# Attention scores of one head pair: 64-row matmuls in three products, or 128-row matmuls on stacked halves

## The chip, the core and the metric

The kernel runs on one core of one Trainium2 chip. TensorE multiplies matrices (a matmul needs a weight load, shown as PEld, and a moving operand), VectorE (DVE) and ScalarE (ACT) do elementwise work and read the results from PSUM, GpSimd (POOL) does a little elementwise work, and SyncE (SP) issues transfers, which 16 DMA engines carry out. Each engine works through its own list of instructions in a fixed order; semaphores make one wait for another. SyncE's list is a queue too: an issue that waits holds up the issues behind it.

The metric is the device time of one execution in microseconds. Executions differ a little: three runs of this kernel gave 2321.94, 2323.30 and 2325.07 us.

## What is computed

The reference is a trunk of two layers over 512 tokens of width 1024. Each layer has a gated feed-forward half step, a mixer, a second feed-forward half step and a gated embedding. The mixer of the first layer is a state-space scan, that of the second is neighbourhood attention on a grid of 8 rows by 64 columns. The change is inside that attention alone:

```
qkv = (h @ w_qkv).reshape(bsz, rows, GRID_W, 3, NA_HEADS, NA_HEAD_DIM)   # 16 heads of 64
q = rmsnorm(qkv[:, :, :, 0], q_norm) * (NA_HEAD_DIM ** -0.5)
k = rmsnorm(qkv[:, :, :, 1], k_norm)
s = q . k  over a window of 8 rows x 32 columns = 256 keys per block of 16 query columns
s = s + bias;  pr = softmax(s);  o = pr . v
```

There are 4 blocks of 16 columns by 8 rows, so 128 queries by 256 keys per block and head. A score is a sum over the 64 elements of a head.

Everything is in 32-bit floats. TensorE is used in a rounded form of them (fp32r), so the kernel splits each operand into a high part (rounded) and a low part (the rest), and adds three products: high with high, high with low, low with high.

## The kernel before

Activations lie with features on the 128 partitions and tokens on the free axis, as 8 tiles of 128 by 512. Weights come in units of 128 by 1024 (512 KB), loaded by SyncE (`load_unit`, L204), split into high and low by ScalarE (L221) and VectorE (L223), and used by `gemm`: 24 matmuls of 128 rows by 512 columns (L278, L281, L282), three products for each of 8 tiles. Up to three units wait as raw loads and up to three are split ahead.

In `attention` two heads share a tile of 128 partitions: head 0 of a pair on partitions 0 to 63, head 1 on 64 to 127. There are eight pairs, numbered j.

`keys` projects the key tiles (four early, four beside the loop), sums their squares (L1135), takes the reciprocal root on VectorE (L1139, on 8 partitions), writes it to DRAM (L1141), brings it back spread over the partitions (L1147), scales the keys (L1148) and splits them into a tile `kn` with a high and a low half (L1150, shown as L303 and L304). `kn` stays in SBUF, in the list `kz`, until its pair is done.

`project(j)` is a generator with four steps. It asks for the bias tables (L1166, two transfers of 384 KB, one for each head), runs the query projection in two halves, scales it (L1173), splits it into `qs[0]` (ScalarE, L1177) and `qs[1]` (VectorE, L1178), and then runs the value projection; beside it stands the reciprocal root of the query's norm (L1184 to L1188).

`attend(j)` runs one pair behind, beside `project(j + 1)`. `scores` takes two blocks of queries at a time and fills two PSUM banks, one for each head (L1209): for each block three products, each for both heads, so 12 matmuls with 64 rows, 128 query columns and 256 keys. The two heads' matmuls alternate in the program and use different rows of the array. `soften` adds the bias (L1219) and does the softmax (L1222 to L1234), `values` turns the values (L1243), `turn` the probabilities (L1252, L1254), and `weigh` multiplies both, with 64 output columns per matmul (L1263).

The order of each engine's list is not the program's. The framework that compiles the kernel places instructions on each engine by a planner: it goes by program order as a priority, by modelled durations and by which operands and tile slots are ready at the modelled time. So SyncE issues the bias of pair 1 in the same breath as that of pair 0, and a score block can be split by work that became ready in the planner's view. Tiles come from pools with a fixed number of slots: `hs` (8, for h, and in this stage for `qs`), `md` (24, of two halves each), `sq` (4), and five plus three PSUM banks.

At the start of the stage the eight tiles of h are parked in DRAM (L133), and fetched again at its end (L139) into the slots that `qs` used.

Of the kernel before, what the change touches and what calls it, by code (L numbers as in the profile page):

```python
# [14 lines left out]
P = 128  # L15
# [55 lines left out]
def trunk(ctx, tc, A, out):  # L71
# [1010 lines left out]
    def attention(norm, nxt):  # L1082
# [9 lines left out]
        def keys(js):  # L1092
# [50 lines left out]
            for i in range(4):  # L1143
                rb = sc()
                for a in range(2):
                    r_ = slice(a * 64, (a + 1) * 64)
                    sy.dma_start(out=rb[r_], in_=rkd[2 * i + a:2 * i + a + 1, :].to_broadcast([64, T]))  # L1147
                v.scalar_tensor_tensor(out=rb, in0=raw[i], scalar=gqk, in1=rb, op0=ALU.mult, op1=ALU.mult)  # L1148
                kn = md(F32R)
                split(kn, rb, None)  # L1150
                kz.append(kn)
                if js[0]:
                    yield
            yield
# [5 lines left out]

        def project(j):

            bias = []
            for a in range(2):
                bt = md().rearrange("p x k -> p (x k)")[:, :768].rearrange("p (x k) -> p x k", x=3)
                sy.dma_start(out=bt, in_=A["bias"][j, :, 3 * a:3 * a + 3, :])  # L1166
                bias.append(bt)
            pt, w = mm_bank(), unit()
            half_gemm(pt, w, 0)
            yield  # L1170
            half_gemm(pt, w, 1)
            qb = t2()
            v.tensor_mul(out=qb, in0=pt, in1=R)  # L1173
            qq = sc()
            s.activation(out=qq, in_=qb, func=AF.Square)
            qs = [bp.tile([P, T], F32R, name=nm("hs"), tag="hs", bufs=8) for _ in range(2)]
            s.copy(out=qs[0], in_=qb)  # L1177
            v.tensor_sub(out=qs[1], in0=qb, in1=qs[0])  # L1178
            yield
            pt, w = mm_bank(), unit()  # L1180
            half_gemm(pt, w, 0)
            pq = px_bank()
            for b in range(4):
                te.matmul(out=pq[:, 2 * b:2 * b + 2], lhsT=qq[:, b * P:(b + 1) * P], rhs=msk[:, M_BLK:M_BLK + P:64],  # L1184
                          start=True, stop=True)
            mq, rq = sm([8]), sm([8])
            v.tensor_scalar(out=mq, in0=pq[:, :8], scalar1=EPS, scalar2=None, op0=ALU.add)
            newton_rsqrt(mq, rq, sm([8]))  # L1188
            yield
            half_gemm(pt, w, 1)  # L1190
            vt = t2()
            v.tensor_mul(out=vt, in0=pt, in1=R)
            made[j] = (bias, qs, kz[j], rq, vt)
            yield

        opr = [None] * 8

        def attend(j):

            bias, qs, kj, rq, vt = made.pop(j)  # L1200
            st, pT = {}, {}
            def scores(bs):

                pscore = [px_bank() for _ in range(2)]
                for n, b in enumerate(bs):
                    for i, (x, y) in enumerate(((0, 0), (0, 1), (1, 0))):
                        for a in range(2):
                            r_ = slice(a * 64, (a + 1) * 64)
                            te.matmul(out=pscore[a][:, n * 256:(n + 1) * 256], lhsT=qs[x][r_, b * P:(b + 1) * P],  # L1209
                                      rhs=kj[r_, y, KC0[b] * 8:KC0[b] * 8 + 256], start=i == 0 and n == 0,  # L1210
                                      stop=i == 2 and n == 1)
                for n, b in enumerate(bs):
                    soften(b, [p[:, n * 256:(n + 1) * 256] for p in pscore])

            def soften(b, pscore):
                x = st[b] = sc()
                for a in range(2):
                    sl = slice(a * 256, (a + 1) * 256)
                    v.scalar_tensor_tensor(out=x[:, sl], in0=pscore[a], scalar=rq[:, 2 * b + a:2 * b + a + 1],  # L1219
                                           in1=bias[a][:, VAR[b], :], op0=ALU.mult, op1=ALU.add)  # L1220
                mx, su = sm([2]), sm([2])
                v.tensor_reduce(out=mx, in_=x.rearrange("p (a k) -> p a k", a=2), axis=AX.X, op=ALU.max)  # L1222
                v.tensor_scalar(out=mx, in0=mx, scalar1=-1.0, scalar2=None, op0=ALU.mult)
# [279 lines left out]
```

## Time and profile before

| what | value |
| --- | --- |
| median of three runs | 2323.3 us (2321.94 to 2325.07) |
| span of the profiled execution | 2323.5 us |
| TensorE busy | 2306.5 us, 99% of the span |
| VectorE busy | 1817.3 us, 78% |
| ScalarE busy | 1181.0 us, 51% |
| score matmuls (L1209) | 192, from 1724.6 to 1868.5 us |
| attention stage | about 1640 to 1890 us |

The page gives only the span for the profiled execution, 2323.5 us; its own device time is not among the three runs listed. The span lies 0.2 us above their median, so nothing but a few tenths can lie around it.

The profile lists, for each engine, the time in which an instruction was running. Matmuls overlap in the array: a matmul of 128 rows by 512 columns lasts 0.39 us from its start to its end, but the next one starts 0.23 us after it. So the cost of a group of matmuls is read from starts: from the start of what stands before the group to the start of what stands behind it. "Idle before" with an arrow names what ended the wait of an engine. The granted clock is the share of its full clock at which TensorE was allowed to run.

### The profile page before, as it was taken

To read this page: it belongs to the slowest core of one execution; us is meant where nothing else is said; L and a number is where in the kernel's file an instruction comes from. 1 tells how busy PE (TensorE), PEld (TensorE's weight loads), DVE (VectorE), ACT (ScalarE), POOL (GpSimd) and SP (SyncE) were. 2 spreads that over 40 slices of the span, in tenths; PEclk is the share of its full clock that TensorE was granted. 3 is DMA by queue.
4 is the path that set the end of the run, shared out by engine and by line. 5 is a ranking of instruction groups with operands and counts; after the bars stand their busy time and mean duration, and the time that the engine had idled before them with its cause. 6 is when DMAs were issued, how large, how long until landed. Compare 5 with 4: busy or idle time off the path is not lost.

```text
span 2323.5 us, 35452 instructions
## 1 busy us (share of the span) xinstructions
PE 2306.5 (99%) x13812; PEld 2027.9 (87%) x13812; DVE 1817.3 (78%) x2621; ACT 1181.0 (51%) x2038; POOL 331.6 (14%) x261
## 2 busy tenths in 40 slices
PE   9999999999999999999999999999999999999999
PEld 7899998788888888999998889999877888999987
DVE  7878868887777858987885897787587769888856
ACT  5434445686667864444445444444446754444452
POOL 0000001265555641000003100000210010000020
PEclk9999999999999999999999999999999999999999
DMA  5323323444444543332223223222433332333232
GB/s 185 118 79 109 105 89 127 138 146 155 148 146 147 173 159 117 102 100 98 90 88 107 100 101 109 87 96 87 147 126 109 108 116 99 105 109 100 82 96 73
DMA packets 99240, 265.97 MB, mean 114 GB/s; under 512 B 12016, under 2 KB 12912, under 8 KB 99072
## 3 DMA queue, kind: packets, MB, share of 16 engines
q1 hardware_dynamic: 98784, 263.57, 34.4%
q8 instruction: 108, 1.77, 0.3%
q14 instruction: 60, 0.49, 0.1%
q10 hardware_dynamic: 288, 0.14, 0.0%
HBM read 253.40 MB, written 10.26 MB: 113 GB/s over the span
## 4 chain that ended last, share of the span: by engine, by line
PE 93%; DVE 3%; ACT 1%; DMA 1%; issue 0%; POOL 0%; SPq 0%; ACTq 0%; POOLq 0%; DVEq 0%
PE ps L278 19%; PE ps L281 19%; PE ps L282 19%; PE ps L510 10%; PE ps L509 10%; PE ps L508 10%; PE ps L879 1%; PE ps L920 1%; PE ps L1263 1%; PE ps L900 1%; PE ps L1209 1%; DVE wl L223 1%; PE ps L1252 1%; PE ps L824 1%; PE ps L835 1%; DVE md L304 0%
## 5 line engine op out<-in xcount | busy, mean ns | idle before, releaser
L278 PE MATMUL ps<-md,wh 128*128 128x512 f32 (+1 forms) x2032 | 801.3, 395 | 0.0
L281 PE MATMUL ps<-md,wh 128*128 128x512 f32 (+1 forms) x2032 | 792.9, 390 | 0.7 <-DVE md L307 0.7
L282 PE MATMUL ps<-md,wl 128*128 128x512 f32 (+1 forms) x2032 | 791.3, 390 | 1.4 <-DVE wl L223 1.4
L221 ACT CAST wh<-wr 128x1024 fp32r<-128x1024 f32 (+2 forms) x395 | 352.0, 892 | 509.5 <-PE ps L281 263.0
L223 DVE TENSOR_TENSOR wl<-wr,wh 128x1024 fp32r<-128x1024 f32 (+2 forms) x395 | 421.2, 1067 | 78.1 <-ACT wh L221 70.0
L282 PEld LDWEIGHTS ps<-md,wl 128*128 128x128 f32 x2032 | 381.7, 188 | 82.6 <-DVE wl L223 2.9
L278 PEld LDWEIGHTS ps<-md,wh 128*128 128x128 f32 x2032 | 382.4, 188 | 75.5 <-issue 2.1
L281 PEld LDWEIGHTS ps<-md,wh 128*128 128x128 f32 x2032 | 382.6, 188 | 72.4 <-DVE md L307 1.6
L221 ACT CAST wh<-md 128x1024 fp32r<-128x1024 f32 x175 | 183.6, 1049 | 321.9 <-PE ps L509 299.7
L332 POOL TENSOR_TENSOR sq<-sq,sq 128x512 f32<-128x512 f32 x71 | 104.2, 1467 | 1645.2 <-ACT sq L328 1640.8
L510 PE MATMUL ps<-sc,wl 128*128 128x256 f32 x980 | 277.5, 283 | 0.8 <-DVE wl L223 0.8
L508 PE MATMUL ps<-sc,wh 128*128 128x256 f32 x980 | 276.9, 283 | 0.8 <-ACT wh L221 0.8
L509 PE MATMUL ps<-md,wh 128*128 128x256 f32 x980 | 277.4, 283 | 0.1
L510 PE MATMUL ps<-md,wl 128*128 128x256 f32 x980 | 277.3, 283 | 0.0
L509 PE MATMUL ps<-sc,wh 128*128 128x256 f32 x980 | 277.3, 283 | 0.0
L508 PE MATMUL ps<-md,wh 128*128 128x256 f32 x980 | 277.2, 283 | 0.0
L514 DVE TENSOR_TENSOR t<-ps,t 128x512 f32<-128x512 f32 x245 | 166.0, 689 | 136.3 <-PE ps L510 135.6
L223 DVE TENSOR_TENSOR wl<-md,wh 128x1024 fp32r<-128x1024 f32 x175 | 213.6, 1221 | 15.7 <-ACT wh L221 15.4
L508 PEld LDWEIGHTS ps<-sc,wh 128*128 128x128 f32 x980 | 187.7, 192 | 4.9 <-ACT wh L221 1.0
L509 PEld LDWEIGHTS ps<-sc,wh 128*128 128x128 f32 x980 | 187.7, 192 | 3.9
L509 PEld LDWEIGHTS ps<-md,wh 128*128 128x128 f32 x980 | 188.0, 192 | 1.6 <-DVE md L472 0.4
L508 PEld LDWEIGHTS ps<-md,wh 128*128 128x128 f32 x980 | 188.0, 192 | 1.3
(208 smaller groups left out, 2904.4 us busy)
## 6 DMA issues: line engine op xcount, KB each, us to landing
wr<-in_w_gw_dram SPq DMA_DIRECT2D x70, 512.0 KB, 3.8
md<-in_w_gw_dram SPq DMA_DIRECT2D x70, 512.0 KB, 4.7
wr<-in_w_in_dram SPq DMA_DIRECT2D x65, 512.0 KB, 3.9
wr<-in_w_dn_dram SPq DMA_DIRECT2D x128, 256.0 KB, 2.6
wr<-in_w_gu_dram SPq DMA_DIRECT2D x32, 512.0 KB, 3.5
hs<-crow SPq DMA_DIRECT2D x64, 256.0 KB, 4.1
wr<-in_w_dn_dram SPq DMA_DIRECT2D x32, 384.0 KB, 3.1
wr<-in_w_qkv_dram SPq DMA_DIRECT2D x24, 512.0 KB, 3.5
```

Of the source, the lines that this page charges most:

```text
L221: splits.append(s.copy(out=hi[:, :n], in_=raw[:, :n]))
L223: v.tensor_sub(out=lo[:, :n], in0=raw[:, :n], in1=hi[:, :n])
L278: m = te.matmul(out=pt, lhsT=hi[:, sl], rhs=part(xp, 0, cols), start=first and k == 0, stop=False)
L281: te.matmul(out=pt, lhsT=hi[:, sl], rhs=part(xp, 1, cols), start=False, stop=False)
L282: gemm.last = te.matmul(out=pt, lhsT=lo[:, sl], rhs=part(xp, 0, cols), start=False, stop=last and k == n - 1)
L332: (v if fast else g).tensor_add(out=self.acc, in0=self.acc, in1=q)
L508: te.matmul(out=o, lhsT=hi[:, sl], rhs=xh, start=j == 0 and kk == 0, stop=False)
L509: te.matmul(out=o, lhsT=hi[:, sl], rhs=xl, start=False, stop=False)
L510: te.matmul(out=o, lhsT=lo[:, sl], rhs=xh, start=False, stop=j == 1 and kk == 3)
L514: v.tensor_add(out=k[to], in0=pt, in1=k[other])
L824: te.transpose(out=pt[:, cs(i)], in_=src[:, cs(c)], identity=ident)
L835: te.matmul(out=pt[:, cs(c)], lhsT=bt[:, dr, cs(c)], rhs=ct_[:, dr, cs(c)], start=True, stop=True)
```

## The change

Each head gets its own pair of operands with all 128 partitions in use.

- The key tile `kn` (high and low half on the free axis) is written to a DRAM tile `kd` by one transfer of 512 KB, and no longer stays in SBUF.
- For each pair and head, `project(j)` makes a tile `qt`: partitions 0 to 63 hold the high part of this head's query, partitions 64 to 127 its low part (two transfers within SBUF of 128 KB). It makes a tile `kt` that holds the head's keys, high and low halves, twice: on partitions 0 to 63 and again on 64 to 127 (two transfers of 256 KB from `kd`). That is eight transfers per pair, issued on SyncE at the end of the step that makes `qs`.
- `scores` runs, for each block and head, two matmuls of 128 rows by 256 columns: the stacked query with the high half of the keys, and with the low half. The sum over 128 rows adds high and low of the query, so all four products are formed, the low with low one included. A pair's two blocks take 8 matmuls where 12 stood.
- The bias tables come as one tile of four tables (in a slot of `md`) and one of two (in a slot of `sq`), where two tiles of three stood.

```
@@ keys
                 kn = md(F32R)
                 split(kn, rb, None)
-                kz.append(kn)
+                kd = dp.tile([P, 2, T], F32, name=nm("kd"))
+                sy.dma_start(out=kd, in_=kn.bitcast(F32))
+                kz.append(kd)
@@ project
-            bias = []
-            for a in range(2):
-                bt = md().rearrange("p x k -> p (x k)")[:, :768].rearrange("p (x k) -> p x k", x=3)
-                sy.dma_start(out=bt, in_=A["bias"][j, :, 3 * a:3 * a + 3, :])
-                bias.append(bt)
+            bt, bu = md().rearrange("p x (y k) -> p (x y) k", y=2), sq().rearrange("p (x k) -> p x k", x=2)
+            sy.dma_start(out=bt, in_=A["bias"][j, :, :4, :])
+            sy.dma_start(out=bu, in_=A["bias"][j, :, 4:, :])
+            bias = [[(bt[:, n] if n < 4 else bu[:, n - 4]) for n in range(3 * a, 3 * a + 3)] for a in range(2)]
...
             s.copy(out=qs[0], in_=qb)
             v.tensor_sub(out=qs[1], in0=qb, in1=qs[0])
+            qk = []
+            for a in range(2):
+                r_ = slice(a * 64, (a + 1) * 64)
+                qt = bp.tile([P, T], F32R, name=nm("hs"), tag="hs", bufs=8)
+                kt = md(F32R)
+                for x in range(2):
+                    c_ = slice(x * 64, (x + 1) * 64)
+                    sy.dma_start(out=qt[c_].bitcast(F32), in_=qs[x][r_].bitcast(F32))
+                    sy.dma_start(out=kt[c_].bitcast(F32), in_=kz[j][r_])
+                qk.append((qt, kt))
             yield
...
-            made[j] = (bias, qs, kz[j], rq, vt)
+            made[j] = (bias, qk, rq, vt)
@@ attend / scores
-                    for i, (x, y) in enumerate(((0, 0), (0, 1), (1, 0))):
-                        for a in range(2):
-                            r_ = slice(a * 64, (a + 1) * 64)
-                            te.matmul(out=pscore[a][:, n * 256:(n + 1) * 256], lhsT=qs[x][r_, b * P:(b + 1) * P],
-                                      rhs=kj[r_, y, KC0[b] * 8:KC0[b] * 8 + 256], start=i == 0 and n == 0,
-                                      stop=i == 2 and n == 1)
+                    for (qt, kt), p in zip(qk, pscore):
+                        for y in range(2):
+                            te.matmul(out=p[:, n * 256:(n + 1) * 256], lhsT=qt[:, b * P:(b + 1) * P],
+                                      rhs=kt[:, y, KC0[b] * 8:KC0[b] * 8 + 256], start=y == 0 and n == 0,
+                                      stop=y == 1 and n == 1)
@@ soften
-                                           in1=bias[a][:, VAR[b], :], op0=ALU.mult, op1=ALU.add)
+                                           in1=bias[a][VAR[b]], op0=ALU.mult, op1=ALU.add)
```

2 lines of the change are left out of this document (1 added, 1 removed).

## The prediction

> **What bounds the kernel now.** I read the page first, then busy times by stretches of the attention stage, then the list of instructions in order of time for TensorE, SyncE and VectorE. The page, with its engine line and its chain of waits:
>
> ```profile
> span 2323.5 us, 35452 instructions
> ...
> PE 2306.5 (99%) x13812; PEld 2027.9 (87%) x13812; DVE 1817.3 (78%) x2621; ACT 1181.0 (51%) x2038; POOL 331.6 (14%) x261
> ...
> PE 93%; DVE 3%; ACT 1%; DMA 1%; issue 0%; POOL 0%; SPq 0%; ACTq 0%; POOLq 0%; DVEq 0%
> ```
>
> The span is 2323.5 us against a median of 2323.3, so the sums below are made on the span and carried over with -0.2. TensorE sets the end: it is busy 99% and holds 93% of the chain. The change touches only the loop over eight head pairs, about 1724 to 1872 us. Stretches of it (columns: length; busy time with count of PE, PEld, DVE, ACT, POOL; granted clock; DMA share; GB/s):
>
> ```profile
> 1724.00:1742.00 18.00, 18.00 (x109) 14.67 (x108) 15.78 (x37) 10.95 (x24) 0.00 (x0) 1.00 0.20 74
> 1742.00:1760.00 18.00, 15.86 (x99) 12.18 (x97) 12.69 (x36) 8.53 (x21) 0.00 (x0) 0.81 0.45 147
> 1760.00:1868.00 108.00, 107.48 (x778) 87.67 (x779) 83.65 (x249) 73.21 (x180) 0.00 (x0) 1.00 0.32 106
> ```
>
> From 1760 on TensorE never rests, so a nanosecond saved on it there is saved at the end. In the first stretch VectorE is nearly full too, and the second has the one hole: TensorE waits for the softmax of the first pair, and the granted clock falls to 0.81.
>
> ```profile
> 1745.83 0.49 PE L1252 MATMUL ps<-msk,sc 128*128 128x128 f32 x2 [2.14 <-ACT sc L1234]
> ```
>
> That hole costs 2.1 us plus 18 x 0.19 = 3.4 us of clock.
>
> **The change part by part: the score matmuls.** Each of the 16 score blocks (eight pairs, two blocks each) has 12 matmuls of 64 rows by 256 columns. They become 8 of 128 rows by 256; the fourth product, low half times low half, rides along. An unbroken block now (start, duration, engine, line, tiles, shape, count):
>
> ```profile
> 1724.10 0.39 PE L281 MATMUL ps<-md,wh 128*128 128x512 f32 x1
> 1724.33 0.39 PE L282 MATMUL ps<-md,wl 128*128 128x512 f32 x1
> 1724.65 0.97 PE L1209 MATMUL ps<-md,hs 64*128 64x256 f32 x12
> 1725.55 0.66 PE L1243 MATMUL ps<-msk,t 128*128 128x128 f32 x4
> ```
>
> From the last projection matmul to what follows the block is 1725.55 - 1724.33 = 1.22 us; less the 0.23 that this matmul holds the array, the block costs 0.99. Twelve matmuls in 0.99 means that the two heads' matmuls already run side by side on the two halves of the rows: one alone could not go at 83 ns, since a full matmul of 256 columns elsewhere is paced like this, first and last of 15:
>
> ```profile
> 299.82 0.28 PE L508 MATMUL ps<-md,wh 128*128 128x256 f32 x1
> ...
> 301.50 0.28 PE L510 MATMUL ps<-md,wl 128*128 128x256 f32 x1
> ```
>
> (301.50 - 299.82) / 14 = 0.12 us. The new block is 8 x 0.12 = 0.96. An unbroken block gains only 0.03. I went through all 16 blocks in order of time and sorted them by what stands beside them.
>
> The Trainium skill (TensorEngine Tiling (Array Packing), Overview) promises up to 2x for a contraction of 64 rows packed two by two, and so speaks against unpacking. By it the old block would be 6 x 0.12 = 0.72, and the change would cost 16 x 0.24 = 3.8 us. The trace's 0.99 says otherwise: what packing saves goes at the edges of the block.
>
> The larger gain is in blocks that the planner's order breaks, because the edges are then paid again, and a piece of one head alone has no partner:
>
> ```profile
> 1768.88 0.62 PE L1209 MATMUL ps<-md,hs 64*128 64x256 f32 x6
> 1769.62 1.97 PE L1263 MATMUL ps<-sc,md 128*64 128x128 f32 x32
> 1771.52 0.62 PE L1209 MATMUL ps<-md,hs 64*128 64x256 f32 x6
> 1772.07 0.66 PE L1243 MATMUL ps<-msk,t 128*128 128x128 f32 x4
> ...
> 1773.59 1.57 PE L1209 MATMUL ps<-md,hs 64*128 64x256 f32 x12
> 1775.09 0.50 PE L278 MATMUL ps<-md,wh 128*128 128x512 f32 x1
> 1775.42 0.39 PE L281 MATMUL ps<-md,wh 128*128 128x512 f32 x1
> ```
>
> Here the weighing of the pair before (L1263) splits a block: 0.74 + 0.55 and an entry of 0.09 are 1.38, against 0.96 and 0.09 for the edge that the weighing keeps: 0.33 gained. Four blocks are of this kind: 1.3 us. The next block (1773.59) ran one head after the other: 1.50, 0.10 at entry, and the matmul after it held 0.10 longer, 1.70 in all, so 0.74 gained. One more is torn by projection matmuls:
>
> ```profile
> 1754.38 0.98 PE L1209 MATMUL ps<-md,hs 64*128 64x256 f32 x6
> 1755.28 0.50 PE L281 MATMUL ps<-md,wh 128*128 128x512 f32 x1
> 1755.62 0.40 PE L282 MATMUL ps<-md,wl 128*128 128x512 f32 x1
> ...
> 1756.18 0.97 PE L1209 MATMUL ps<-md,hs 64*128 64x256 f32 x6
> 1757.08 0.50 PE L281 MATMUL ps<-md,wh 128*128 128x512 f32 x1
> ```
>
> Two pieces of 0.10 + 0.90 + 0.10 are 2.20; 1.24 gained. And one sits behind the hole, at a low clock:
>
> ```profile
> 1746.25 1.01 PE L1209 MATMUL ps<-md,hs 64*128 64x256 f32 x5
> 1747.19 0.69 PE L1252 MATMUL ps<-msk,sc 128*128 128x128 f32 x2
> 1747.81 1.01 PE L1209 MATMUL ps<-md,hs 64*128 64x256 f32 x6
> 1748.75 3.67 PE L1263 MATMUL ps<-sc,md 128*64 128x128 f32 x31
> ```
>
> Eleven matmuls take 0.94 + 0.94; eight full ones at half pace are about 8 x 0.24 = 1.9, so after the twelfth some 0.4 is gained. The other nine blocks gain 0.03 each, 0.3. Sum: 1.3 + 0.7 + 1.2 + 0.4 + 0.3 = 3.9, taken as -4.0. The least is 16 x 0.03 = 0.5, if the new order breaks no block that isn't cheap anyway; the most 5.5, if two of the nine that I count as whole are of the kind at 1773.
>
> **The transfers.** Per pair four transfers of 128 KB (query halves, within SBUF) and four of 256 KB (keys, from DRAM) are added, 1.5 MB, and once per key tile a write of 512 KB to DRAM: 16.8 MB and 72 issues on SyncE's queue. The bias tables move from two transfers of 384 KB to one of 512 and one of 256, the same bytes: nothing. VectorE, ScalarE and GpSimd keep their work: nothing. Two queries' tiles more per pair in the pool of eight, and the bias in the pool of four: both turn over within two pairs, and the park-and-fetch of h at the end waits, as now, for the last scores. Nothing, unless the order puts a fetch first.
>
> What the queue and the engines of DMA carry now, over 1724 to 1868, with times to landing:
>
> ```profile
> q1 hardware_dynamic: 5408, 15.22, 31.7%
> ...
> wr<-in_w_qkv_dram SPq DMA_DIRECT2D x8, 512.0 KB, 3.8
> ```
>
> 15.22 MB in 144 us at 31.7% is 333 GB/s for engines that run full; 16.8 MB more is 50 us of the 144, so 67% busy: weights land later, but they are asked for several units of 5.5 us (24 x 0.23) ahead, and that hides it. In the steady state the query halves must land before the scores. For the fifth pair:
>
> ```profile
> 1797.16 0.68 DVE L1178 TENSOR_TENSOR hs<-t,hs 128x512 fp32r<-128x512 f32 x1
> ```
>
> ```profile
> 1801.08 0.33 SPq L204 DMA_DIRECT2D wr<-in_w_qkv_dram  x1
> ```
>
> ```profile
> 1806.94 0.62 PE L1209 MATMUL ps<-md,hs 64*128 64x256 f32 x6
> ```
>
> Low half done at 1797.8, scores at 1806.9: 9.1 us. Four issues of 0.5 (2.08 / 4, the bias transfers below) and some 3 us to land, a little under the 3.8 of a load four times as large, make 5. If they stand behind the weight load that SyncE holds until 1801.1, they land at 1806: still in time. Behind that wait stand further loads and biases, which have a pair's time to spare. Cost: 0; its other end is a late landing of 2 to 3 us in most pairs.
>
> The first pair has less. Its keys and its queries (SyncE, then VectorE):
>
> ```profile
> 1704.83 4.92 SPq L1147 DMA_DIRECT2D sc<-rkd  x8
> 1709.84 1.31 SPq L204 DMA_DIRECT2D wr<-in_w_qkv_dram  x2
> 1711.21 2.08 SPq L1166 DMA_DIRECT2D md<-in_bias_dram  x4
> 1719.44 5.04 SPq L204 DMA_DIRECT2D wr<-in_w_qkv_dram  x2
> ```
>
> ```profile
> 1716.26 0.68 DVE L304 TENSOR_TENSOR md<-sc,md 128x512 fp32r<-128x512 f32 x1
> ...
> 1717.55 0.69 DVE L1178 TENSOR_TENSOR hs<-t,hs 128x512 fp32r<-128x512 f32 x1
> ```
>
> The low half is done at 1718.2 and the scores start at 1724.65, 6.4 us later. In the queue before the query halves stand what is there now (two loads, four biases: 2.6 MB) and four key writes and the first key stack, 3.1 MB more. At 333 GB/s the 6.3 MB, with the query halves, take 18.9 us from about 1711: landing near 1730, an estimate, 5.4 us late. The scale broadcasts that VectorE waits for (L1147) are all issued by 1709.8 and stay ahead of the key writes, so nothing on VectorE waits behind these. TensorE has 36 projection matmuls of the second pair left (8.3 us) that can go first, if the fixed order puts them there. Cost between 0 and 5.4 plus a clock drop of 3.4; I take 1.5, nearer to nothing because of that filler.
>
> Sum: 2323.5 - 4.0 + 1.5 = 2321.0.
>
> **The rivals.** (a) The first stack is late and TensorE's order does not fill the gap: for it, 2.1 us of waiting already brought the clock to 0.81; against it, the filler. +5.4 + 3.4 - 4.0: 2328. It decides from about 2 us of idle on. The Trainium skill (SBUF — State Buffer, the port table by partition range and the part on two halves) says that 64 partitions reach 8 of 16 ports, 196 GB/s, and that two halves serialize; by it the 1.57 MB of a pair's stacks take 8.0 us instead of 4.7 and the rival costs 3.3 more, 2332; no transfer to 64 partitions here is long enough to show it. (b) Query halves are late in most pairs, 2 us each in six: +12 - 4, 2331. For it, SyncE waits in order; against it, the 9 us. (c) The gain is taken back by softmax on VectorE and ScalarE (84 and 73 of 108 us busy, against it): 2323.5. (d) The later first scores shift the hole at 1743 away: -4.0 - 2.1 - 3.4, 2314. (e) The change doesn't do what it says, because unbroken packed blocks already cost the same and the new order has few breaks: -0.5 + 1.5, 2324.5.
>
> **How the numbers follow.** About 0.2% (4.6 us) is what a measurement of this kernel can tell from no change: 2318.7 to 2327.9. Chances: forecast 0.36, of it 0.15 below 2318.7; (a) 0.20, of it 0.15 above 2327.9; (b) 0.10; (c) 0.10; (d) 0.17, all faster; (e) 0.07, of it 0.01 slower. Faster 0.15 + 0.17 = 0.32; slower 0.15 + 0.10 + 0.01 = 0.26; same 0.42. The forecast's own range is 2316 to 2325; with (d) and (a) it reaches from 2312 to 2331.
>
> **What would show it.** Score blocks of 8 at a pitch of 0.12 with no longer neighbours; score time by block near 0.96 whether broken or not. Rival (a): an idle of TensorE before the first scores that ends on a transfer into the query tile, and a clock below 1 behind it. (b): the same wait in later pairs. (d): no hole near 1743 and a clock of 1.00 from 1742 to 1760. I am wrong if full matmuls of 256 columns go slower than 0.12 here, or if SyncE's waits hold the weights.

## The result and the profile after

The changed kernel takes 2335.51 us in the median (2332.19 to 2336.22, four runs), against 2323.68 (2321.94 to 2325.07) for the kernel before in the same runs: a ratio of 1.0049, 95% interval 1.0038 to 1.0061. It is about 12 us slower. The prediction said 2321.0, with a range of its own from 2316 to 2325, and from 2312 to 2331 with two of its rivals.

The page of the changed kernel (engines with busy time, share and count; the queue that SyncE and ScalarE use, in packets, MB and share of the DMA engines; the chain of waits):

```profile
span 2333.3 us, 35464 instructions
...
PE 2308.1 (99%) x13748; PEld 2034.9 (87%) x13748; DVE 1818.3 (78%) x2621; ACT 1179.9 (51%) x2038; POOL 331.6 (14%) x261
...
q1 hardware_dynamic: 105056, 280.35, 36.8%
...
PE 93%; DVE 4%; ACT 2%; DMA 1%; issue 0%; POOL 0%; ACTq 0%; POOLq 0%; SPq 0%; DVEq 0%
```

TensorE's count fell by 64 (sixteen calls of `scores`, four matmuls fewer in each), VectorE and ScalarE do the same work as before. The span grew by 9.8 us, 2333.3 against 2323.5. In the chain of waits VectorE and ScalarE each hold 1% more; the DMA engines hold no more than before.

Stretches of 18 us of the attention stage of the changed kernel (columns as in the prediction: length; busy time with count of PE, PEld, DVE, ACT, POOL; granted clock; DMA share; GB/s):

```profile
1724.00:1742.00 18.00, 18.00 (x95) 14.94 (x94) 14.68 (x33) 8.84 (x18) 0.00 (x0) 1.00 0.84 219
1742.00:1760.00 18.00, 14.59 (x97) 12.66 (x95) 12.06 (x36) 11.04 (x30) 0.00 (x0) 0.81 0.84 254
1760.00:1778.00 18.00, 14.07 (x95) 11.95 (x94) 13.20 (x36) 8.73 (x20) 0.00 (x0) 0.91 0.33 108
1778.00:1796.00 18.00, 18.00 (x126) 15.10 (x125) 13.17 (x42) 11.71 (x31) 0.00 (x0) 1.00 0.65 211
1796.00:1814.00 18.00, 16.51 (x90) 13.63 (x90) 13.18 (x35) 11.36 (x30) 0.00 (x0) 1.00 0.74 233
1814.00:1832.00 18.00, 18.00 (x125) 15.32 (x124) 13.29 (x34) 11.42 (x27) 0.00 (x0) 1.00 0.67 178
1832.00:1850.00 18.00, 15.14 (x99) 13.10 (x98) 11.96 (x40) 10.51 (x29) 0.00 (x0) 0.81 0.74 217
```

Before, one stretch had a hole, and from 1760 on TensorE never rested. Now four of seven have holes, and in three of them the clock is below 1. No other engine is full there: VectorE is busy 12 to 15 of 18 us. The DMA engines are at 0.33 in one stretch with a hole and at 0.84 in the first, which has none.

What TensorE waited for in the stage, first before, then after (what waited, on what; us in total, times, longest):

```profile
PE ps L1252 <- ACT sc L1234: 2.3, 2, 2.1
```

```profile
PE ps L1262 <- ACT sc L1244: 11.7, 7, 2.9
```

It is one wait in both: the turning of the probabilities (L1252 before, L1262 after) waits for ScalarE's last step of the softmax. No scores and no projection matmul waits for a transfer. VectorE and ScalarE, too, wait in this stage (1715 to 1890 us) only for each other and for TensorE, never for a transfer. The sum over the two traces is: idle 11.7 - 2.3 = +9.4; clock 18 x (0.19 + 0.09 + 0.19) = 8.46 against 3.42 before, +5.0; scores -4.0 (from the first experiment below). Together +10.4, against 9.8 of span.

The score matmuls themselves, TensorE in order of time after the change (start, duration, engine, line, tiles, shape, count):

```profile
1727.42 0.39 PE L278 MATMUL ps<-md,wh 128*128 128x512 f32 x1
1727.65 0.64 PE L1219 MATMUL ps<-md,hs 128*128 128x256 f32 x4
1728.12 0.40 PE L281 MATMUL ps<-md,wh 128*128 128x512 f32 x1
...
1796.72 0.39 PE L282 MATMUL ps<-md,wl 128*128 128x512 f32 x1
1796.95 1.11 PE L1219 MATMUL ps<-md,hs 128*128 128x256 f32 x8
1797.90 0.60 PE L1253 MATMUL ps<-msk,t 128*128 128x128 f32 x4
```

Eight take 1797.90 - 1796.95 = 0.95 us, and half a call 1728.12 - 1727.65 = 0.47: 0.12 us for each, whole or broken, and the neighbours keep their 0.23. Only behind a hole are they slower (eight take 1.76 us at 1773, with a granted clock of 0.59 from 1772.9 to 1774.8); the sum above counts that as clock. That part went as predicted.

How a hole comes about is seen where VectorE's, ScalarE's and TensorE's lists are read together (here for the hole at 1832; brackets: idle before and what ended it):

```profile
1817.28 1.45 PE L1219 MATMUL ps<-md,hs 128*128 128x256 f32 x8
1818.56 0.60 PE L1253 MATMUL ps<-msk,t 128*128 128x128 f32 x4
...
1825.62 0.69 DVE L1203 TENSOR_TENSOR t<-ps,rt 128x512 f32<-128x512 f32 x1 [3.23 <-PE ps L282]
1826.23 0.47 DVE L1229 SCALAR_TENSOR_TENSOR sc<-ps,sm,md 128x256 f32<-128x256 f32 x1
...
1831.57 0.60 PE L1262 MATMUL ps<-msk,sc 128*128 128x128 f32 x4
1831.92 0.48 PE L282 MATMUL ps<-md,wl 128*128 128x512 f32 x1
...
1834.70 0.51 ACT L1244 ACTIVATE sc<-sc,sm 128x256 f32<-128x256 f32 x1
1835.26 1.11 PE L1262 MATMUL ps<-msk,sc 128*128 128x128 f32 x4 [2.86 <-ACT sc L1244]
```

The scores are done at 1818.6. VectorE's list has the scaling of the next pair's values (L1203) ahead of the softening of these scores (L1229), so it stands idle for 3.2 us until the value projection ends, and softens them from 1826.2 on. On TensorE's list three, ten and one projection matmuls stand between the four groups of turnings: between the third and the fourth there is one, and TensorE waits 2.9 us. It is the order of the lists that makes this wait, not a transfer that came late.

That order can be read from the kernels as they are built, without a time. Here are the lists of TensorE for one or two pairs in the middle of the stage (G projection, q query norms, S scores, V values turned, T probabilities turned, W weighing, each with its count):

```
before  S6 W16 S6 V4 G6 S12 V4 G12 q4 G4 T4 G1 T4 G16 T4 G7 T4 S6 W16
after   S4 G2 S4 G3 V4 G11 q4 G26 T4 G2 T12 S8 W16
        S8 V4 G12 S8 V4 G17 q4 G23 T4 G3 T4 G5 T8 S8 W16
```

Before, the four groups of turnings of a pair are kept apart by 24 projection matmuls, in which the softmax catches up. After the change the projection matmuls have gone ahead, and up to 12 turnings stand in a row (14 in the first pair). Below, "clump" is a group of eight or more, leaving out the last pair, which has one in nearly every kernel. Before has none, after has four. Of the 11.7 us of waits, 8.9 lie in the first, second and fourth pair, each of which has a clump; 2.9 are the hole at 1832, in the fifth pair, which has none but little filler; and the clump of the seventh pair has no wait. So a clump is a common form of the harm, not its only one.

### The profile page after: what moved, and what is told of

Its sections match the earlier page's. It is cut to its first block, busy times and chain, and to the rows that moved or that the text cites. A ratio compares the mean times of both kernels' runs of the same rounds, so it can differ in the third digit from the quotient of the medians.

```text
span 2333.3 us, 35464 instructions
## 1 busy us (share of the span) xinstructions
PE 2308.1 (99%) x13748; PEld 2034.9 (87%) x13748; DVE 1818.3 (78%) x2621; ACT 1179.9 (51%) x2038; POOL 331.6 (14%) x261
## 4 chain that ended last, share of the span: by engine, by line
PE 93%; DVE 4%; ACT 2%; DMA 1%; issue 0%; POOL 0%; ACTq 0%; POOLq 0%; SPq 0%; DVEq 0%
PE ps L278 19%; PE ps L281 19%; PE ps L282 18%; PE ps L510 10%; PE ps L509 10%; PE ps L508 10%; PE ps L1273 1%; PE ps L1219 1%; PE ps L920 1%; DVE wl L223 1%; PE ps L879 1%; PE ps L900 1%; DVE t L756 1%; PE ps L824 1%; PE ps L1262 1%; PE ps L835 1%
```

## The experiments

Theories named in the expectations: W, the scores wait for their stacks; C, the added traffic holds up other transfers; S, the bias tables' new slots; P, the two tiles more in the pool of eight; Q, the time that the planner reckons for SyncE's one queue changes the order of the other engines' lists. Q1 is that queue waiting in order behind the query halves, Q2 the sum of time reckoned for all issues.

**The shape alone.** The 128-row matmuls run on the tiles where they lie; no key write, no stack transfer. So the sums run over both heads, and the scores are not the reference's.

```
-                kd = dp.tile([P, 2, T], F32, name=nm("kd"))
-                sy.dma_start(out=kd, in_=kn.bitcast(F32))
-                kz.append(kd)
+                kz.append(kn)
...
+            qk = [(qs[a], kz[j]) for a in range(2)]
```

> The new score matmuls alone: 8 of 128 rows, but on the tiles that lie there (the query's high part for head 0, its low part for head 1, the key tile as it is); the key write and all stacking transfers are left out, so the scores are sums over both heads and not the reference's. The bias tables as in the changed kernel. Theory W (the scores now wait for stacked tiles, the planner places work around that wait, and softmax comes too late for the turning matmuls): no wait is left, so the gain of the blocks shows, 3.7 us, about 2320. Theory C (traffic of the transfers slows loads): also about 2320. Theory S (the bias in other slots, or the blocks themselves, upset the order): 2328 or more.

Measured: 2318.95 us, ratio 0.9980 (0.9971 to 0.9990). Its waits and its stretch with the hole:

```profile
PE ps L1251 <- ACT sc L1233: 2.6, 1, 2.6
```

```profile
1742.00:1760.00 18.00, 15.40 (x107) 13.21 (x106) 13.38 (x39) 10.78 (x26) 0.00 (x0) 0.91 0.47 145
```

One wait is left, as before. Added up over all groups of score matmuls in the two traces, from the start of the matmul in front of a group to the start of the one behind it, the sixteen calls take 22.2 us against 26.1. In one group more a projection matmul stands in front here (0.23), so some 4 us are gained, the number of the prediction. The shape is worth some 4.5 us in the median; the whole change loses 16.6 on top of it.

**The bias tables alone**, on the kernel before (the six bias lines of the change and nothing else).

> The kernel before with the bias tables as in the changed kernel (four in a slot of one pool, two in a slot of another), nothing else. Theories W and C: no difference, 2322 to 2326. Theory S: 2328 or more.

Measured: 2323.56, ratio 1.0000 (0.9990 to 1.0009). Theory S falls.

**The transfers with the old matmuls.** All transfers, but to the partitions on which the data lies already; the 64-row matmuls read the copies.

```
-                    sy.dma_start(out=qt[c_].bitcast(F32), in_=qs[x][r_].bitcast(F32))
-                    sy.dma_start(out=kt[c_].bitcast(F32), in_=kz[j][r_])
+                    sy.dma_start(out=qt[c_].bitcast(F32), in_=qs[a][c_].bitcast(F32))
+                    sy.dma_start(out=kt[c_].bitcast(F32), in_=kz[j][c_])
...
```

> The changed kernel with the old score matmuls: the same number, sizes and queue places of transfers, but they copy query parts and keys to the same partitions, and the 12 matmuls of 64 rows read the copies. The scores wait as in the changed kernel and the blocks cost as before. Theory W: slower than before by the holes alone, 2335.5 plus 3.7, about 2339 (2334 to 2342). Theory C: about 2339 too. Theory S: 2324 to 2328 would speak for it if the bias run is slow.

Measured: 2335.88, ratio 1.0050 (1.0035 to 1.0065). The loss is there without the new matmuls. About 2339 was expected, as the old matmuls cost some 4 us more; it lies at the low end of the range given. Its list is not that of the changed kernel (clumps of 14, 8 and 8), so the parts do not simply add up.

**Stacks that nobody reads.** The kernel before with every transfer of the change; its 64-row matmuls read the tiles in place.

```
-                kz.append(kd)
+                kz.append((kn, kd))
...
-            made[j] = (bias, qk, rq, vt)
+            made[j] = (bias, qs, kz[j][0], rq, vt)
...
```

> The kernel before with all the transfers and the bias of the changed kernel, but the scores read the old tiles: nobody waits for the stacks, while the bytes, the issues on SyncE and the slots are as in the changed kernel. Theory W: 2322 to 2327, no wait, no holes. Theory C: 2330 or more, as the traffic is all there. Theory S: 2328 or more.

Measured: 2333.92, ratio 1.0043 (1.0028 to 1.0058). Its wait:

```profile
PE ps L1263 <- ACT sc L1245: 9.7, 6, 3.4
```

The same wait of turnings for softmax as in the changed kernel, though no instruction reads a stack. W falls; the built list has three clumps (of 16, 8 and 8).

**Slots.** The stacked queries live in a slot of `md` instead of two of `hs`.

```
-            qk = []
+            qk, qm = [], md(F32R)
...
-                qt = bp.tile([P, T], F32R, name=nm("hs"), tag="hs", bufs=8)
+                qt = qm[:, a, :]
```

> The changed kernel with both heads' stacked queries in one slot of the pool of 24 in place of two of the pool of eight, so that the pool of eight serves four pairs again and not two. The runs before left out a wait on the stacks (unread stacks cost 10.5 us too) and the bias (no difference). Theory P (slots of the pool of eight hold back the projection of the pair after next): the holes go, about 2320. Theory Q (SyncE's one queue: 72 more issues, some of which wait, push back what stands behind them where the planner orders the work): 2330 or more. Theory C (the traffic itself): 2330 or more.

Measured: 2331.75, ratio 1.0034 (1.0022 to 1.0046). Some 4 us of the loss go; the greater part stays, and so P is at most a small part.

**One kind of transfer at a time.** Query halves alone (32 issues, keys in place), then key writes and key stacks alone (40 issues, queries in place). In both the scores are not the reference's.

```
-                kt = md(F32R)
+                kt = kz[j]
...
-                    sy.dma_start(out=kt[c_].bitcast(F32), in_=kz[j][r_])
```

> The changed kernel with the query transfers only: four per pair, 32 in all, 4.2 MB; the key write and the key stacks are left out and the matmuls read the key tile as it lies, so the scores are not the reference's. Theory Q: SyncE gets 32 issues more in place of 72, and TensorE's list comes out nearly as in the run without transfers (16 matmuls between the second and third turning, not a clump), so 2318 to 2322. Theory P: the pool of eight is shared as in the changed kernel, 2328 or more. Theory C: a quarter of the bytes, 2319 to 2323.

```
-                qt = bp.tile([P, T], F32R, name=nm("hs"), tag="hs", bufs=8)
+                qt = qs[a]
...
-                    sy.dma_start(out=qt[c_].bitcast(F32), in_=qs[x][r_].bitcast(F32))
```

> The changed kernel with the key transfers only: eight writes and four reads per pair, 40 issues, 12.6 MB; the query stacks are left out (high part of both heads for head 0, low part for head 1), so the scores are not the reference's. Theory Q: the key transfers wait for slots and for the key writes on the same queue, TensorE's list is disturbed again but less than with both; 2322 to 2332. Theory C: three quarters of the bytes, 2328 to 2333. Theory P: the pool of eight is as before, about 2320.

Measured: 2319.35, ratio 0.9981 (0.9972 to 0.9991), and 2319.42, ratio 0.9981 (0.9971 to 0.9991). Each alone costs nothing against the shape (2318.95), both together 16.6 us: the loss is no sum of two prices. Neither list has a clump. P falls here: the query halves fill the pool of eight as in the change, and nothing is lost.

**Another queue for all of it.** The whole computation; all 72 transfers are issued by GpSimd.

```
-                sy.dma_start(out=kd, in_=kn.bitcast(F32))
+                g.dma_start(out=kd, in_=kn.bitcast(F32))
...
-                    sy.dma_start(out=qt[c_].bitcast(F32), in_=qs[x][r_].bitcast(F32))
-                    sy.dma_start(out=kt[c_].bitcast(F32), in_=kz[j][r_])
+                    g.dma_start(out=qt[c_].bitcast(F32), in_=qs[x][r_].bitcast(F32))
+                    g.dma_start(out=kt[c_].bitcast(F32), in_=kz[j][r_])
```

> The changed kernel, complete, with the key writes and all stacking transfers issued from GpSimd's queue, which has next to nothing in this stage; SyncE's queue is as before the change. Same bytes over the same DMA engines. Theory Q: no queue is held up, TensorE's list is nearly that of the run without transfers from the second pair on; 2318 to 2324 (the first stack can still be late). Theory C: 2330 or more, as the traffic is all there. Theory P: 2328 or more.

Measured: 2324.49, ratio 1.0004 (0.9994 to 1.0013). Its waits and its first stretch:

```profile
PE ps L1219 <- DMA md<-kd: 4.4, 1, 4.4
PE ps L1262 <- ACT sc L1244: 2.4, 1, 2.4
```

```profile
1724.00:1742.00 18.00, 13.63 (x63) 11.48 (x63) 9.11 (x19) 5.74 (x11) 4.12 (x8) 0.81 0.77 213
```

The same data are moved in the same stage, and 11 of the 12 us are gone: the traffic (C) is not the cause of the loss. The list has no clump, and only one softmax wait is left. In its place the first scores wait 4.4 us for their keys, and the clock falls to 0.81: rival (a) of the prediction, on this queue.

**Parts on GpSimd's queue.** Query halves there, keys on SyncE; then the key stacks there, the rest on SyncE.

```
-                    sy.dma_start(out=qt[c_].bitcast(F32), in_=qs[x][r_].bitcast(F32))
+                    g.dma_start(out=qt[c_].bitcast(F32), in_=qs[x][r_].bitcast(F32))
```

> The changed kernel, complete, with only the query transfers (32 of the 72) issued from GpSimd's queue; key writes and key stacks stay on SyncE's. All bytes over the same DMA engines. The score and turning matmuls then stand on TensorE in the very order of the run with key transfers alone (2319.4). Theory Q (SyncE's queue, as the planner reckons with it, sets the harmful order): 2318 to 2322, and the first score block not late by more than 2 us, since the key stacks have SyncE's queue. Theory C (traffic): 2330 or more.

```
-                    sy.dma_start(out=kt[c_].bitcast(F32), in_=kz[j][r_])
+                    g.dma_start(out=kt[c_].bitcast(F32), in_=kz[j][r_])
```

> The changed kernel, complete, with the key stacks (32 of the 72) issued from GpSimd's queue and the query transfers and key writes on SyncE's. Theory Q: as good from the second pair on, but the first key stack is late as in the run with everything on GpSimd's queue: 2319 to 2325. Theory C: 2330 or more.

Measured: 2322.28 (2320.18 to 2328.28), ratio 0.9998 (0.9989 to 1.0006), and 2327.38, ratio 1.0017 (1.0007 to 1.0026). Two stretches of the first:

```profile
1724.00:1742.00 18.00, 17.10 (x93) 14.20 (x92) 13.71 (x32) 9.69 (x22) 2.06 (x4) 1.00 1.03 272
1742.00:1760.00 18.00, 15.44 (x108) 13.18 (x107) 14.18 (x41) 10.86 (x26) 2.06 (x4) 0.91 0.75 216
```

With the query halves on GpSimd the list is the very one of the run with keys alone, without a clump. The DMA engines are full in the first stretch and TensorE loses 0.9 us there, in one wait for a key stack. This is level with the kernel before. But it is 2.9 us slower than keys alone (2319.42) with the same list for TensorE, so the added transfers can cost a few us in themselves; which waits these are was not worked out. The second lies above the 2319 to 2325 expected, though its list has no clump either: its first scores wait 4.0 us for a query stack, which is on SyncE's queue, not for the keys on GpSimd's, while the DMA share of that stretch is 1.03.

**Key stacks asked for early.** All on SyncE, the key stacks of a pair at the start of `project(j)`, ahead of the query projection.

```
+            kts = []
+            for a in range(2):
+                kt = md(F32R)
+                for x in range(2):
+                    sy.dma_start(out=kt[x * 64:(x + 1) * 64].bitcast(F32), in_=kz[j][a * 64:(a + 1) * 64])
+                kts.append(kt)
...
+                kt = kts[a]
...
-                    sy.dma_start(out=kt[c_].bitcast(F32), in_=kz[j][r_])
```

> The changed kernel, complete, all 72 transfers on SyncE's queue, but a pair's key stacks are asked for ahead of its bias and query projection, so that they need not stand behind the query transfers, which wait for the split. Theory Q1 (what harms is the waiting in order: keys, biases and weights behind query transfers that wait): 2318 to 2323. Theory Q2 (what harms is the sum of the time that the planner reckons for 72 issues more in one queue): clumps remain in TensorE's list, 2327 or more.

Measured: 2324.85, ratio 1.0005 (0.9996 to 1.0014). This lies between the two expectations. Most of the loss is gone, and the list keeps two clumps (of 16 and 8). So where the issues stand in SyncE's queue counts too.

**Queries stacked by the engines.** ScalarE and VectorE write each half to the partitions where it is wanted; no query transfers.

```
+                s.copy(out=qt[r_], in_=qb[r_])
+                v.tensor_sub(out=qt[o_], in0=qb[r_], in1=qt[r_])
...
-                    sy.dma_start(out=qt[c_].bitcast(F32), in_=qs[x][r_].bitcast(F32))
```

> The changed kernel, complete, with the queries stacked by the engines that split them: ScalarE rounds each head's 64 partitions into its tile, VectorE writes the low part to the other 64 partitions of that tile; twice the instructions there (+0.6 us on ScalarE, +0.7 on VectorE per pair), no query transfers; the key transfers stay on SyncE's queue. Theory Q: as the run with key transfers alone, less what VectorE's extra time costs: 2319 to 2324. Theory C: three quarters of the bytes, 2319 to 2324 too.

Measured: 2324.09, ratio 1.0000 (0.9991 to 1.0009). Better than the change by 11 us, but some 5 us short of keys alone. The split now takes twice as many instructions, each on half the partitions, and the list has two clumps, with no wait of TensorE in front of them; where the 5 us go was not worked out.

**Number of issues, or bytes.** The stacks that nobody reads again, with 128 and with 256 of the 512 columns moved: the same 72 issues behind the same producers on SyncE, a quarter and a half of the bytes. The edit for a quarter:

```
-                sy.dma_start(out=kd, in_=kn.bitcast(F32))
+                sy.dma_start(out=kd[:, :, :128], in_=kn[:, :, :128].bitcast(F32))
...
+                    sy.dma_start(out=qt[c_, :128].bitcast(F32), in_=qs[x][r_, :128].bitcast(F32))
+                    sy.dma_start(out=kt[c_, :, :128].bitcast(F32), in_=kz[j][1][r_, :, :128])
...
```

> The run with unread stacks (2333.9) again, with every transfer cut to 128 of its 512 columns: the same 72 issues on SyncE behind the same producers, a quarter of the bytes, old 64-row matmuls on the tiles in place. In the order of TensorE's instructions as it is built the turnings stand spread as in the kernel before, except one group of eight late. Theory 'number of issues, or waits in order': the loss stays, 2331 to 2335. Theory 'bytes that the planner reckons in SyncE's queue': nearly all of the loss goes; scores cost as before, one clump is worth 0 to 3 us: 2323 to 2327.

> The same with 256 of 512 columns: half the bytes, the same 72 issues and waits. In its order three pairs have eight turnings in a row. By issues or waits: 2331 to 2335. By bytes: between the quarter and the whole, each clump some 2 to 3 us with its clock loss now and then: 2326 to 2331.

And the keys alone with 72 issues instead of 40, each stack cut in two:

```
-                qt = bp.tile([P, T], F32R, name=nm("hs"), tag="hs", bufs=8)
+                qt = qs[a]
...
-                    sy.dma_start(out=kt[c_].bitcast(F32), in_=kz[j][r_])
+                    for y in range(2):
+                        sy.dma_start(out=kt[c_, y].bitcast(F32), in_=kz[j][r_, y])
```

> Keys only, as in the run with key transfers alone (2319.4), but each key stack cut into two transfers along the high and low part, so that SyncE has 72 issues as the whole change has, with the bytes of the 40; the queries are read in place, so its scores are not the reference's. Number of issues: the loss of the whole change comes back, 2330 to 2335. Bytes, or the query transfers that wait in order: as with 40 issues, 2318.5 to 2320.5.

Measured: 2323.49, ratio 0.9997 (0.9988 to 1.0006); 2324.93, ratio 1.0003 (0.9994 to 1.0012); 2319.55, ratio 0.9983 (0.9974 to 0.9992). The waits of the first:

```profile
PE ps L1263 <- ACT sc L1245: 2.4, 2, 2.1
```

The number of issues is not it: with half the bytes the 10 us are all but gone, and 72 issues with the keys' bytes cost nothing. The bytes in SyncE's queue decide, and not in proportion; the half came out below what I had expected. One thing moved with the bytes: SyncE's own list, in which from the second pair on the four key stacks and the four query halves stand in two groups, where with the full bytes (the run with unread stacks) they stand in turn for the first three pairs.

**Engine-stacked queries, key stacks on GpSimd**, tried as a version to beat both kernels.

```
...
-                    sy.dma_start(out=kt[c_].bitcast(F32), in_=kz[j][r_])
+                    g.dma_start(out=kt[x * 64:(x + 1) * 64].bitcast(F32), in_=kz[j][r_])
```

> The whole computation: the queries' halves are written to their stack by ScalarE and VectorE as in the engine-stacked run (2324.1), and the key stacks are asked for on GpSimd's queue; SyncE keeps the key writes. Its order has spread turnings for five pairs of eight. If only the order counts: 2319.5 to 2322, as the shape alone plus up to 2.5 us for ScalarE and VectorE working on half the partitions twice. If GpSimd's keys land 4 us late for the first scores, as in the run with key stacks on GpSimd (2327.4), that and the clock add 5 to 7: 2325 to 2328.

Measured: 2322.31 (2318.77 to 2325.24), ratio 0.9992 (0.9982 to 1.0002). The interval touches 1: no gain is shown.

**The order changed, the transfers left as they are.** The changed kernel with all transfers on SyncE, and edges of order on TensorE: parts of the next projections (three matmuls each) stand behind given turnings.

```
+                b = turned.get(behind[k - 4 * half]) if behind else None
+                with tc.issue_after(b.ins) if b else ExitStack():
+                    gemm(pt, w, norm.pairs[k:k + 1], first=k == 0, last=k == 7, off=k)
...
+            half_gemm(pt, w, 0, [(j - 2, 1), (j - 2, 1), (j - 2, 2), (j - 2, 2)])
...
+            half_gemm(pt, w, 1, [None, None, (j - 1, 0), (j - 1, 1)])
...
```

> The changed kernel with all 72 transfers on SyncE as they are, and eight edges of order per pair: the last six projection matmuls of a pair's values stand behind the first and second turning, the twelve of the next query half behind the second and third. In TensorE's order most groups of 8 to 16 turnings are so broken up by 4 to 9 projection matmuls. Theory 'the order alone makes the loss': TensorE finds work while it waits for softmax, idle falls from 11.7 us to some 3 to 6 and the clock comes back: 2319.5 to 2324. Theory 'the transfers on SyncE hold up the engines in a way that the order only follows': the waits move to the projection matmuls or the scores, 2330 to 2336.

In the second, with `behind` given at two other places and none for the values:

```
+            half_gemm(pt, w, 0, [(j - 2, 1), (j - 2, 1), (j - 2, 1), (j - 2, 2)])
...
+            half_gemm(pt, w, 1, [(j - 2, 3), None, None, None])
...
```

> The same with other edges: three of the next query half's groups of three projection matmuls behind the second turning, one behind the third, and one of the second half behind the fourth; the values' projection is left free. Two to three pairs keep eight turnings in a row, with 8 to 12 projection matmuls ahead of them. By the order: 2319.5 to 2324; by the transfers: 2330 to 2336.

Measured: 2327.03 (2323.91 to 2330.07), ratio 1.0015 (1.0006 to 1.0024), and 2331.47, ratio 1.0036 (1.0024 to 1.0048). The first falls between the two expectations; the second falls in that of the transfers, and its list kept four clumps. Four of the stretches and TensorE's longest waits of the first:

```profile
1724.00:1742.00 18.00, 11.83 (x65) 9.77 (x64) 15.79 (x37) 9.24 (x22) 0.00 (x0) 0.88 0.87 219
1742.00:1760.00 18.00, 18.00 (x117) 15.30 (x115) 12.53 (x36) 10.78 (x26) 0.00 (x0) 0.93 0.65 199
1760.00:1778.00 18.00, 18.00 (x128) 15.47 (x126) 14.63 (x42) 13.03 (x32) 0.00 (x0) 1.00 0.78 227
...
1832.00:1850.00 18.00, 18.00 (x126) 15.21 (x126) 13.73 (x40) 12.91 (x32) 0.00 (x0) 1.00 0.67 187
```

```profile
PE ps L1265 <- DVE sm L1241: 5.1, 1, 5.1
PE ps L1265 <- ACT sc L1247: 3.8, 1, 3.8
```

With the same transfers on the same queue, the holes at 1768 and 1832 are gone, and the clock there is 1.00: in the medians 8.5 us come back in the first and 4.0 in the second by changing the order. It is the order of all lists that changed: the edges stand on TensorE, but SyncE's list came out otherwise too (for the third pair the four key stacks now stand in a group ahead of the query halves). What is left in the first sits in two waits. One stands in front of eight turnings in a row, in the first pair. Before the second, VectorE and SyncE in order of time (first SyncE, then VectorE):

```profile
1796.74 0.59 SPq L1191 DMA_DIRECT2D md<-kd  x1
1797.38 1.24 SPq L1147 DMA_DIRECT2D sc<-rkd  x2
...
1803.26 0.75 DVE L1148 SCALAR_TENSOR_TENSOR sc<-md,gqk,sc 128x512 f32<-128x512 f32 x1 [3.31 <-DMA sc<-rkd]
1803.93 0.16 DVE L1241 RECIPROCAL sm<-sm 128x2 f32<-128x2 f32 x1
```

Here a transfer does hold an engine up: the scales of a key tile (L1147) were issued right behind a stack transfer and landed late, VectorE waited 3.3 us for them with a step of the softmax (L1241) behind it in its list, and TensorE waited for that. So SyncE's queue can also cost by real waits; in the changed kernel itself the trace shows no such wait.

## Why the prediction was wrong

**The score matmuls (-4.0): right.** Eight matmuls at 0.12 us, the same whether broken or not, no longer neighbours; some 4 us less over the sixteen calls, and 2318.95 us where the shape stands alone. The rule of the Trainium skill (TensorEngine Tiling (Array Packing), Overview) that 64-row matmuls packed in pairs run up to twice as fast would, at its full 2x, have made this a loss of 3.8 us; some 4 us were gained. In the trace of the kernel before, in the block at 1724.65, the pairs start 0.115 us apart, as fast as one full matmul, so inside a group packing does what the rule says; but some 0.1 us more each at the entry, behind the first pair and at the exit eat it in groups so short.

**The first stack late (+1.5): it did not come.** The stacks of the first pair were late as estimated, and the filler hid it, as hoped: the last of their transfers lands at 1730.3, against the 1730 of the prediction. The planner runs the first head's scores at 1727.65 instead of 1724.65, puts 19 projection matmuls behind them and the second head's at 1732.46, all without a wait. That the 1730 came out is in part luck: from 1709 on only one weight load and one bias transfer stand ahead of the stacks in SyncE's list, where the prediction counted two loads and four bias transfers. Rival (a), 2328, did not happen in the changed kernel; the runs with transfers on GpSimd's queue show its mechanism (4.4 and 4.0 us of wait).

**The transfers in the steady state (cost 0): the step that failed.** The working asked when the bytes land and who waits for them, and found 9 us of room; that was right, no TensorE instruction waits for a stack in the changed kernel. It took the order of the other engines' lists as given ("VectorE, ScalarE and GpSimd keep their work: nothing"): they keep their work, but not its order. The front part of this document says that the planner orders by modelled durations and by when operands are ready at the modelled time; the prediction used this only as "if the fixed order puts them there". Together the 72 transfers changed that order on TensorE and VectorE, and the change costs 16.6 us over the shape alone. By the two traces 11.7 - 2.6 = 9.1 of that is idle and 8.46 - 1.62 = 6.8 is clock, in holes of one kind. The two signs of being wrong that the prediction named, slower full matmuls and weights held up by SyncE's waits, did not come; it had no sign for this.

**"Nothing, unless the order puts a fetch first" (slots): nearly right.** Bias tables 0.0; the slots of the stacked queries some 4 us in the run that moved them, which also changes the order, and nothing in the run with query halves alone, which fills them.

**The rivals.** (b), waits on query halves: no such wait. (c) names the place, softmax, but as a limit of VectorE and ScalarE and with a gain merely taken back; these engines are no fuller than before, and what was lost is four times that gain. (d), the hole shifted away: it is still there at 1743 (2.2 us, clock 0.81 behind it). (e): the gain from the shape is real. None of them was that the planner's order breaks, which is the case that came.

**What is shown and what is not.** Shown: the loss needs both kinds of transfer on SyncE with their full bytes, at the places where the change has them; it comes without any reader of the stacks; in the changed kernel neither TensorE nor VectorE nor ScalarE waits for a transfer in this stage; the same traffic from another queue does not bring the loss; and changing the order of the lists, with the same transfers on the same queue, gives back 8.5 of the 16.6 us in one run and 4.0 in another. That the planner's modelled time for SyncE's queue is what turns the order is concluded from these, since the profile shows no modelled times. How the other 8 us divide between what is still badly ordered, on VectorE's list too, and real waits behind stack transfers stays open. The count of clumps is a sign, not a measure: kernels without one lie at 2319 to 2327 us, those with two at 2322 to 2325, those with three or four at 2327 to 2336.

## What to carry to other kernels

Where a planner orders the engines' lists, a transfer that hides perfectly can still cost: price it also by what its bytes in one queue may do to the order of everything else, and read the built order of the bounding engine beside the diff before trusting a sum of parts. When a large loss shows up as waits on an engine with spare time, look for filler that has moved: here the projection matmuls that used to stand between the turnings. The quickest tests are to make the transfers unread, to cut their bytes with the count kept, and to issue them from another queue.

## What the runs showed of the hardware that was not expected

**The clock falls after short waits.** A wait of 2.9 us that ends at 1835 goes with a granted clock of 0.81 over the 18 us from 1832 on, as the 2.1 us did before; the shape alone had 2.6 us and 0.91. The two waits of 1.2 and 0.3 us near 1812 left 1.00. One wait of 2.4 us, in the run with the key stacks on GpSimd's queue (1742 to 1760), also left 1.00. So a hole of 2 to 3 us mostly cost 1.6 to 3.4 us more than itself here, once nothing, and not by its length; the 1.2 and 0.3 us cost nothing visible.

**The time to land did not go by the queue that issues.** Issues from 1724 to 1868 us (count, KB each, median us from issue to landing): the changed kernel, all transfers on GpSimd's queue, the query halves alone there, and the key stacks alone there.

```profile
md<-kd SPq DMA_DIRECT2D x28, 256.0 KB, 5.2
...
hs<-hs SPq DMA_DIRECT2D x28, 128.0 KB, 3.1
```

```profile
md<-kd POOLq DMA_DIRECT2D x28, 256.0 KB, 6.6
hs<-hs POOLq DMA_DIRECT2D x28, 128.0 KB, 4.8
```

```profile
md<-kd SPq DMA_DIRECT2D x28, 256.0 KB, 7.5
...
hs<-hs POOLq DMA_DIRECT2D x28, 128.0 KB, 6.7
```

```profile
md<-kd POOLq DMA_DIRECT2D x23, 256.0 KB, 4.3
...
hs<-hs SPq DMA_DIRECT2D x28, 128.0 KB, 4.2
```

The first two alone would say that GpSimd's queue lands 1.4 and 1.7 us later. But key stacks took 4.3 us from GpSimd's queue and 7.5 from SyncE's in the other two. What stands beside a transfer differs from run to run, so an effect of the queue by itself is not shown.

**Full DMA engines did not slow TensorE by themselves.** With a DMA share of 1.03 over 18 us TensorE was busy 17.1 of 18 us at a clock of 1.00 (query halves on GpSimd's queue, first stretch), and the 0.9 us missing are one wait for a key stack.
